# A hybrid decoder layer on one core: the sums of w_down's quarters put in other places, and the output projection's first two tiles written together

## The chip, the cores and the metric

The kernel runs on one core of a Trainium2 chip. The metric is device time in microseconds (us) of the whole launch; the kernel before was run three times. Every time in this document that is not a run's time comes from one profiled execution. Engines: TensorE (PE, matrix products), VectorE (DVE), ScalarE (ACT), GpSimd (POOL) and SyncE (SP). SP, ACT and POOL can each issue DMAs.

## The reference

One layer over 512 tokens of 2048 features, all in float32. Three sub-layers each add to the residual `x`; the last is a gated feed-forward layer with 5632 inner features:

```python
h = rms_norm(x, g_mix)
# h @ w_in -> sparse attention group (8 heads) and gated linear attention group (4 heads)
x = x + jnp.concatenate([o_nsa, o_gla], axis=-1) @ w_out
x = x + cross_attention(rms_norm(x, g_cross), rms_norm(mem, g_mem)) @ w_co   # 4 heads, 256 memory tokens
hf = rms_norm(x, g_ffn)
gg, uu = jnp.split(hf @ w_gu, 2, axis=-1)
return x + (jax.nn.silu(gg) * uu) @ w_down
```

## The kernel before

**Numbers and products.** Every float32 operand of a large product is split into a high and a low part (`split`, lines 153 to 160: a cast on ACT, a subtraction on DVE), and a product is three matmuls (`mm3`): high by high, high by low, low by high. A 128x512 matmul advances PE by about 0.23 us.

**Stages.** In order of time: keys and values of the memory (0 to 50 us); the input projection, its value columns first (`natural`, to 167 us), then tiles of 128 columns (`in_tile`), with the linear attention heads (`gla_head`) beside them, the compressed blocks (`compress_unit`, about 340 to 500 us) and the sparse heads (`nsa_head`, to 765 us); the output projection (`w_out`, 16 tiles, to 940 us); cross attention and its output `w_co` (to 1100 us); gate and up in eleven blocks of 512 inner features (1100 to 1930 us); down in four steps (to the end). The last two use a seven-product scheme of Strassen's kind, which is why sums of weight blocks are wanted.

**Weights.** In the first half `Weights` loads 1024 columns (512 KB) on SP into one of two raw tiles `w`, ACT casts it into one of three tiles `wh`, DVE makes `wl`. In gate and up a load is 768 KB (`weights_1`) or 512 KB (`weights_2`) into one of three tiles `raw`; DVE sums parts of it and ACT and DVE split it into tiles `qh` and `ql` (five and four). Each block of gate and up has two phases of eight steps `kp`; the finished block before is turned (`turn`, called after steps 2 and 4 of the second phase) and stored to DRAM by ACT's queue.

**Sums of w_down.** `w_down` lies in DRAM as quarters of 22 pieces of 512 KB. The tiles `td` in DRAM hold two sums of quarters per piece; the third step of down needs them first, at 2098 us. `add_quarters` makes them by DMA alone, on POOL's queue: a plain copy from DRAM to DRAM (line 143), then an accumulating copy onto it (line 141), 88 DMAs in all. Each waits for the last matmul written before its turn.

**What sets the order.** `Flows` is a list of generators for the small work. `flows.tick()` is called every few matmuls of the large projections; it counts `now` up and starts each entry of `marks` whose tick has come. The 88 sums have ticks from 70 to 576, 5.75 apart. The compiler's scheduler then orders each engine's instructions by priority; an engine takes its own in that order.

Of the kernel before, what the change touches and what calls it, by code (L numbers as in the profile page):

```python
# [19 lines left out]
KT = D // 128  # L20
# [8 lines left out]
NK = NF // 2  # L29
# [12 lines left out]

W_SUM, W_NORM, W_LEVEL = 3, 2, 2

FIRST_SUM, LAST_SUM = 70, 576

SV = {}
_n = 0
# [9 lines left out]
def hybrid_block(ctx: ExitStack, tc: tile.TileContext, x_t, mem_t, sv, cmat, umask, w_a, w_r67, w_v, w_vg, w_v3,  # L58
                 w_vsw, w_gk2, w_c1, w_c2, w_out, w_cq, w_ck, w_cv, w_co, w_gu, w_down, y_t):
    nc = tc.nc  # L60
    V, S, G, PE = nc.vector, nc.scalar, nc.gpsimd, nc.tensor
# [23 lines left out]
    def bank(tag):  # L85
        return psp.tile([128, 512], F32, name=tag, tag=tag, bufs={"mm": 3, "s": 2, "t": 2, "o": 1}[tag])
# [3 lines left out]
    def row(tag, dt=F32):  # L90
        return sb([128, 512], tag, BUFS[tag], dt)

    last_mm = [None]

    def mm(*args, **kw):
        last_mm[0] = PE.matmul(*args, **kw)  # L96

    class Flows:


        def __init__(self):
            self.now, self.live, self.marks = 0, [], []
# [27 lines left out]
    flows = Flows()  # L130
# [5 lines left out]
    def add_quarters(j, accumulate):  # L136
        dst = [td[i % NK][:, 1024 * (i // NK):1024 * (i // NK) + 1024] for i in (j, j - NK)]

        def go():
            if accumulate:  # L140
                i = G.dma_start(dst[0], dst[1] if j >= NK else w_down[1, j], accum_op=OP.add, max_dma_last_dim=2048)
            else:
                i = G.dma_start(dst[0], w_down[0 if j >= NK else 3, j % NK])
            tc.add_manual_dep(i.ins, last_mm[0].ins.name,
                              mybir.DependencyInfo(mybir.DependencyClass.Sync, mybir.DependencyReason.DATA),
                              reason="in its turn")
        return go

    for j in range(2 * NK):
        for k in range(2):  # L150
            flows.marks.append((FIRST_SUM + (2 * j + k) * (LAST_SUM - FIRST_SUM) // (4 * NK), add_quarters(j, k)))

    def split(hi, lo, src, gain=None):

# [7 lines left out]
    def split_row(src, gain=None, tag="X"):  # L162
        pair = row(tag, F32R), row(tag, F32R)
        split(*pair, src, gain)
        return pair

    class Weights:


        def __init__(self, src, cols, cut=1024, ahead=400, raws=(), step=1024):  # L170
            self.src, self.cols, self.cut, self.step, self.raws, self.parts = src, cols, cut, step, raws, []
            if ahead:
                with tc.high_priority(offset=ahead):
                    while len(self.parts) * cut < cols:
                        self.load()
# [22 lines left out]
    def mm3(ps, lhs, rhs, start, stop, again=False):  # L198
        mm(ps, lhs[0], rhs[0], start=start, stop=False, skip_group_check=again)
        mm(ps, lhs[0], rhs[1], start=False, stop=False, skip_group_check=again)  # L200
        mm(ps, lhs[1], rhs[0], start=False, stop=stop, skip_group_check=again)
# [13 lines left out]
    def vec(name, i=0, p=slice(0, 128)):  # L215
        a = SV[name][0] + i
        return vecs[p, a:a + 1]
# [65 lines left out]
    def project(w, src, cols=T, m=128):  # L283
        ps = bank("mm")
        for kt in range(len(src)):
            mm3(ps[:m, :cols], w(m * kt, m), src[kt], start=kt == 0, stop=kt == len(src) - 1)
            if kt % (2 * T // cols) == 1:
                flows.tick()
        return ps[:m, :cols]
# [106 lines left out]
    for kq in range(4):  # L396
# [6 lines left out]
        for k in range(4):  # L403
            kt = 4 * kq + k
# [3 lines left out]
            for h in range(4):  # L408
                mm3(acc_k[h // 2][:, MEM * (h % 2):MEM * (h % 2) + MEM], wk(512 * k + 128 * h, 128), mg[kt],
                    start=kt == 0 and h % 2 == 0, stop=kt == KT - 1 and h % 2 == 1)  # L410
# [53 lines left out]
    def in_tile(n):  # L464
        return project(Weights(w_a[n], 2048), xg)
# [176 lines left out]
    for h in range(GH):  # L642
        qk = []
        flows.start(gla_head(h, qk))
        q, k = row("Q"), row("Q")
# [107 lines left out]
    for b in range(2):  # L753
        for kv in range(2):
            pair = compress_blocks(us, "pe_k", 2 * b + kv)
            ps = in_tile(12 + 2 * b + kv)
# [7 lines left out]
    def nsa_head(h, ps):  # L764
# [89 lines left out]
        for b in range(2):  # L854
            pt = sb([128, 1280], "PH", PTB, F32R), sb([128, 1280], "PL", PTB, F32R)

            def turn(j):
                n = 128 * (NT - j)
                tp = bank("t")
                for i in range(j, NT):  # L860
                    PE.transpose(tp[:, 128 * (i - j):128 * (i - j) + 128],  # L861
                                 ps_[b][:, POFF[i] + 128 * j:POFF[i] + 128 * j + 128], ident)
                split(*part(pt, TOFF[j], n), tp[:, :n])

            def weigh(j):
                n = 128 * (NT - j)
                mm3(o[:, 128 * j:], part(vsw[j], 256 * b + 128 * kv, 128), part(pt, TOFF[j], n),
                    start=False, stop=b == 1 and j == NT - 1)

            turn(0)  # L870
            yield 2
            if b == 0:
                o = bank("o")
                mm(o, vc[:, 128 * kv:128 * kv + 128], pcs, start=True, stop=False)
            for j in range(1, NT):
                turn(j)
                weigh(j - 1)
                yield 2
            weigh(NT - 1)
# [32 lines left out]
    for n in IN_ORDER:  # L912
        ps = in_tile(16 + n)
# [5 lines left out]
    ps = [bank("mm") for _ in range(2)]  # L919
# [14 lines left out]
    mixp = [split_row(mix[k]) for k in MIX_ORDER]  # L934
# [4 lines left out]
        xs.append(t)  # L939
    ss = row("ss")  # L940
    x1g, x1d = [], []
    for m in range(KT):
        ps = project(Weights(w_out[m], 2048), mixp)
        V.tensor_add(xs[m], ps, xs[m])
        if m % 3 == 0:
            x1d.append(dram.tile([128, 512 * min(3, KT - m)], F32, name="x1", tag="x1", bufs=6))
        G.dma_start(x1d[-1][:, 512 * (m % 3):512 * (m % 3) + 512], xs[m])
        if m == 0:
            S.activation(ss, xs[m], AF.Square)
        else:  # L950
            sq = row("n")
            S.activation(sq, xs[m], AF.Square)
            V.tensor_add(ss, ss, sq)
        x1g.append(split_row(xs[m], vec("g_cross", m)))
# [74 lines left out]
    ps = project(Weights(w_cq[0], 2048), x1g)  # L1029
# [6 lines left out]
    def sb1(tag, dt=F32):  # L1036
        return pool1.tile([128, COLS2.get(tag, 512)], dt, name=tag, tag=tag, bufs=BUFS2[tag])
# [10 lines left out]
    def wide_weights(src, ahead):  # L1048
        with tc.high_priority(offset=ahead):
            raw = sb1("raw")  # L1050
            nc.sync.dma_start(raw, src)
            w = [split_cols(raw, 1024 * i, 1024) for i in range(2)]
        return lambda a, n: part(w[a // 1024], a % 1024, n)
# [11 lines left out]
    ws = [wide_weights(w_co[0], 40)]  # L1065
# [39 lines left out]
    for m in range(KT):  # L1105
        xr = x1[m]
        if m < 4:
            ps = ps4[m]
        else:
            ps = bank("mm")  # L1110
# [80 lines left out]
    def turn(hs, n, k, tag="s"):  # L1191
        def go():
            ps = [bank(tag), bank(tag)]
            for f in range(2):
                c = 256 * k + 128 * f
                for i in range(NT):
                    PE.transpose(ps[f][:, 128 * i:128 * i + 128], hs[i][:, c:c + 128], ident)  # L1197

            e, o, a, b = [sb1("T2") for _ in range(4)]
            S.copy(e, ps[0])  # L1200
            S.copy(o, ps[1])
            x, y = slice(0, 256), slice(256, 512)
            V.tensor_sub(a[:, x], e[:, y], o[:, y])
            V.tensor_sub(b[:, x], e[:, x], e[:, y])
            V.tensor_sub(a[:, y], a[:, x], e[:, x])
            V.tensor_add(b[:, y], o[:, x], a[:, y])
            d = hd[n // 3].rearrange("q (p c) -> q p c", p=7)
            c = 512 * (n % 3) + 256 * k
            S.dma_start(d[:, 0, c:c + 256], e[:, x])
            for p, t in ((1, o), (3, a), (5, b)):  # L1210
                S.dma_start(d[:, p:p + 2, c:c + 256], t.rearrange("q (p c) -> q p c", p=2))
        return go

    rc2 = []
# [2 lines left out]
    for n in range(NB):  # L1217
# [18 lines left out]
        if hs:  # L1236
            extra = {2: [turn(hs, n - 1, 0)], 4: [turn(hs, n - 1, 1)]}
# [278 lines left out]
```

## Time and profile before

| | |
|---|---|
| Runs | 2368.25, 2364.55, 2366.92 us; median 2366.92 |
| Profiled execution | 2365.85 us, its span 2364.1 us, mean granted clock 0.992 |
| PE busy | 2304.2 us, 97% of the span, 10954 matmuls |
| DVE, ACT, POOL busy | 71%, 50%, 6% |
| DMA | 421.34 MB, mean 178 GB/s |
| PE waits longest | 14.0 us at 1067 us, 8.1 at 782, 6.1 at 144, 5.7 at the start |

PE is busy nearly all of the time, so a shorter time must come from the stretches in which it idles, or in which its clock is at the lower of its two levels (2.4 and 1.2 GHz). The granted clock of a stretch is a mean: 0.83 over 20 us is 6.8 us at half speed.

### The profile page before, as it was taken

The numbers are of one execution on the slowest core, as the hardware profiler recorded it, in microseconds if no ns is written. First come the engines' busy times: TensorE is split into PE (matmuls) and PEld (weight loads), VectorE is DVE, ScalarE is ACT, GpSimd is POOL, SyncE is SP. The second block draws the span as 40 slices with busy tenths as digits, with TensorE's granted clock in tenths as the row PEclk, the third lists the DMA queues.
The fourth block names the chain that finished last, engine by engine and source line by source line (L and its number), as shares of the span: only waits on it lengthen the run. The fifth ranks groups of instructions, "written<-read, shape, count | busy, mean of one in ns | idle before, by whom it ended". The sixth has DMA issues, their size and how long they took to land.

```text
span 2364.1 us, 29618 instructions
## 1 busy us (share of the span) xinstructions
PE 2304.2 (97%) x10954; PEld 1915.9 (81%) x10954; DVE 1672.1 (71%) x2522; ACT 1185.6 (50%) x1787; POOL 133.4 (6%) x187
## 2 busy tenths in 40 slices
PE   8989999999999899979999999999999999999999
PEld 7788887878888788767888888888888888888887
DVE  6637776556778334478887888788878886785685
ACT  6623444446667223465554555455544556444542
POOL 0010111101112111010000000000000000000000
PEclk9999999999999999999999999999999999999999
DMA  7575446655546776265454455435544578676773
GB/s 240 159 184 139 120 133 181 181 147 143 148 121 192 222 193 185 75 196 170 145 177 144 142 174 169 158 130 171 174 155 132 170 277 327 234 249 230 251 249 143
DMA packets 131682, 421.34 MB, mean 178 GB/s; under 512 B 13488, under 2 KB 33968, under 8 KB 127312
## 3 DMA queue, kind: packets, MB, share of 16 engines
q1 hardware_dynamic: 82048, 325.05, 41.2%
q0 software_dynamic: 26064, 70.00, 12.8%
q10 hardware_dynamic: 23424, 24.39, 2.9%
q8 instruction: 86, 1.41, 0.2%
q14 instruction: 60, 0.49, 0.1%
HBM read 376.92 MB, written 84.67 MB: 195 GB/s over the span
## 4 chain that ended last, share of the span: by engine, by line
PE 88%; DMA 5%; DVE 3%; ACT 2%; issue 1%; SPq 0%; ACTq 0%; DVEq 0%; POOL 0%; POOLq 0%
PE mm L96 47%; PE t L96 15%; PE s L96 14%; PE o L96 10%; DVE wl L157 1%; ACT wh L156 1%; DMA w<-w_v 1%; PE s L1197 1%; PE t L861 1%; DMA w<-w_c 1%; DMA w<-w_a 1%; DMA st<-x_t 1%; DMA st<-spill 0%; ACT P L156 0%; DMA P<-h 0%
## 5 line engine op out<-in xcount | busy, mean ns | idle before, releaser
L156 ACT CAST qh<-raw 128x1024 fp32r<-128x1024 f32 (+1 forms) x520 | 505.7, 980 | 532.6 <-PE o L96 178.9
L157 DVE TENSOR_TENSOR ql<-raw,qh 128x1024 fp32r<-128x1024 f32 (+1 forms) x520 | 584.5, 1131 | 158.0 <-PE mm L96 50.4
L96 PE MATMUL mm<-qh,P 128*128 128x512 f32 x1540 | 535.7, 390 | 0.0
L96 PE MATMUL mm<-X,wh 128*128 128x512 f32 x1568 | 496.7, 397 | 10.1 <-ACT X L156 8.1
L96 PE MATMUL t<-qh,P 128*128 128x512 f32 x968 | 335.7, 392 | 14.0 <-ACT qh L156 14.0
L96 PEld LDWEIGHTS mm<-X,wh 128*128 128x128 f32 x1568 | 289.7, 189 | 66.3 <-ACT X L156 8.5
L96 PEld LDWEIGHTS mm<-qh,P 128*128 128x128 f32 x1540 | 289.5, 188 | 60.5 <-DVE T L1336 0.2
L157 DVE TENSOR_TENSOR wl<-w,wh 128x1024 fp32r<-128x1024 f32 (+2 forms) x154 | 184.5, 1200 | 183.1 <-ACT wh L156 182.5
L96 PE MATMUL mm<-X,wl 128*128 128x512 f32 x784 | 308.9, 394 | 1.8 <-DVE wl L157 1.7
L96 PE MATMUL mm<-ql,P 128*128 128x512 f32 x770 | 300.6, 390 | 0.8 <-DVE ql L157 0.8
L156 ACT CAST wh<-w 128x1024 fp32r<-128x1024 f32 (+2 forms) x154 | 158.2, 1029 | 258.9 <-PE mm L96 164.7
L96 PE MATMUL s<-qh,P 128*128 128x512 f32 x704 | 245.1, 393 | 0.7 <-ACT qh L156 0.7
L96 PEld LDWEIGHTS t<-qh,P 128*128 128x128 f32 x968 | 181.9, 188 | 51.5 <-ACT qh L156 14.5
L96 PE MATMUL t<-ql,P 128*128 128x512 f32 x484 | 188.5, 389 | 0.0
L96 PE MATMUL o<-qh,P 128*128 128x512 f32 x484 | 187.8, 390 | 0.0
L96 PEld LDWEIGHTS mm<-X,wl 128*128 128x128 f32 x784 | 148.1, 189 | 34.5 <-DVE wl L157 3.5
L96 PEld LDWEIGHTS mm<-ql,P 128*128 128x128 f32 x770 | 144.8, 188 | 31.7 <-DVE ql L157 1.9
L96 PEld LDWEIGHTS s<-qh,P 128*128 128x128 f32 x704 | 132.5, 189 | 28.4 <-ACT qh L156 1.7
L96 PE MATMUL s<-ql,P 128*128 128x512 f32 x352 | 138.2, 393 | 0.1
L1139 DVE TENSOR_TENSOR raw<-raw 128x1024 f32<-128x1024 f32 x88 | 106.5, 1220 | 16.9 <-DMA raw<-w_gu 16.8
L96 PE MATMUL mm<-wh,X 128*128 128x512 f32 (+1 forms) x320 | 101.1, 367 | 7.7 <-ACT wh L156 6.5
L96 PEld LDWEIGHTS o<-qh,P 128*128 128x128 f32 x484 | 91.1, 188 | 18.8
(395 smaller groups left out, 3099.9 us busy)
## 6 DMA issues: line engine op xcount, KB each, us to landing
raw<-w_gu SPq DMA_DIRECT2D x88, 768.0 KB, 4.2
raw<-w_gu SPq DMA_DIRECT2D x88, 512.0 KB, 3.5
raw<-w_down SPq DMA_DIRECT2D x88, 512.0 KB, 4.6
td<-w_down POOLq DMA_DIRECT2D x66, 512.0 KB, 5.4
w<-w_a SPq DMA_DIRECT2D x60, 512.0 KB, 4.4
raw<-td SPq DMA_DIRECT2D x22, 1024.0 KB, 4.8
h<-T ACTq DMA_DIRECT2D x66, 256.0 KB, 3.7
w<-w_out SPq DMA_DIRECT2D x32, 512.0 KB, 4.5
```

What stands on the lines that cost most here:

```text
L96: last_mm[0] = PE.matmul(*args, **kw)
L156: S.copy(hi, src)
L157: V.tensor_sub(lo, src, hi)
L861: PE.transpose(tp[:, 128 * (i - j):128 * (i - j) + 128], ps_[b][:, POFF[i] + 128 * j:POFF[i] + 128 * j + 128], ident)
L1139: V.tensor_sub(raw[:, 0:1024], raw[:, 0:1024], raw[:, 512:1536])
L1197: PE.transpose(ps[f][:, 128 * i:128 * i + 128], hs[i][:, c:c + 128], ident)
```

## The change

The 88 sums no longer stand at even distances. 70 of them go into four stretches of ticks: 24 in 112 to 222, 6 in 254 to 300, 22 in 330 to 420 and 18 in 470 to 576. The other 18 are issued in gate and up, one by each of the first 18 calls of `turn`: a pair (copy, then accumulating copy) for each of nine blocks. Such a sum waits for the turn's first subtraction on DVE instead of a matmul. Besides, the first two tiles of the output projection are written as 15 steps of the first, 15 of the second, then the last step of each.

```diff
-FIRST_SUM, LAST_SUM = 70, 576
+SUMS = ((112, 222, 12), (254, 300, 3), (330, 420, 11), (470, 576, 9))
...
-        def go():
+        def go(when=None):
...
-            tc.add_manual_dep(i.ins, last_mm[0].ins.name,
+            tc.add_manual_dep(i.ins, (when or last_mm[0]).ins.name,
...
-    for j in range(2 * NK):
-        for k in range(2):
-            flows.marks.append((FIRST_SUM + (2 * j + k) * (LAST_SUM - FIRST_SUM) // (4 * NK), add_quarters(j, k)))
+    sums = [add_quarters(j, k) for j in range(2 * NK) for k in range(2)]
+    for a, b, n in SUMS:
+        flows.marks += [(a + i * (b - a) // (2 * n), sums.pop(0)) for i in range(2 * n)]
...
+            self.done = False
...
+
+    ws = [Weights(w_out[m], 2048) for m in range(2)]
+    begun = [bank("mm") for _ in ws]
+    for m in (0, 1, 0, 1):
+        for kt in range(KT - 1) if not ws[m].done else (KT - 1,):
+            mm3(begun[m], ws[m](128 * kt, 128), mixp[kt], start=kt == 0, stop=kt == KT - 1)
+            if kt % 2:
+                flows.tick()
+        ws[m].done = True
     for m in range(KT):
-        ps = project(Weights(w_out[m], 2048), mixp)
+        ps = begun[m] if m < 2 else project(Weights(w_out[m], 2048), mixp)
...
-            V.tensor_sub(a[:, x], e[:, y], o[:, y])
+            h = V.tensor_sub(a[:, x], e[:, y], o[:, y])
...
+            if sums:
+                sums.pop(0)(h)
```

POOL's order where the sparse heads end and the output projection begins, before; L959 and L960 reload the keys and values of the memory for cross attention, L947 stores the first sums of the residual:

```order
L930 DMA KS<-spill 128x512
L959 DMA st<-spill 128x512
L960 DMA st<-spill 128x512
L143 DMA td<-w_down 128x1024 x2
L141 DMA td<-td 128x2x512 x2
L143 DMA td<-w_down 128x1024
L959 DMA st<-spill 128x512
L960 DMA st<-spill 128x512
L141 DMA td<-td 128x2x512
L143 DMA td<-w_down 128x1024
L947 DMA x_7170<-KV 128x512 x2
```

The same place on POOL now (these lines are 10 further down in the changed kernel):

```order
L903 DMA st<-spill 128x512
L931 DMA KS<-spill 128x512
L969 DMA st<-spill 128x512
L970 DMA st<-spill 128x512
L969 DMA st<-spill 128x512
L970 DMA st<-spill 128x512
L143 DMA td<-w_down 128x1024
L957 DMA x_7215<-KV 128x512 x2
L141 DMA td<-td 128x2x512
L957 DMA x_7215<-KV 128x512
```

The five sums that stood between the two pairs of reloads are gone from there.

The end of POOL's order now, from the reloads of the residual (L1096) to the last instructions; before, nothing followed the fifteen accumulating DMAs onto `hT`:

```order
L1096 DMA P<-x_8224 128x512
L1139 DMA hT<-C 128x512 x15
L143 DMA td<-w_down 128x1024
L141 DMA td<-td 128x2x512
L143 DMA td<-w_down 128x1024
L141 DMA td<-td 128x2x512
L143 DMA td<-w_down 128x1024
L141 DMA td<-td 128x2x512
L143 DMA td<-w_down 128x1024
L141 DMA td<-td 128x2x512
```

Nine such pairs stand there, the only work of POOL in gate and up.

PE's order at the output projection before: `mm_7119`, `mm_7189` and `mm_7261` are the banks of the first, second and third tile, `X_7070` is the high part of the last of the 16 inputs:

```order
L96 MATMUL mm_7189<-X_7066,wl_7185 128x512
L96 MATMUL mm_7261<-X_7010,wh_7250 128x512
L96 MATMUL mm_7261<-X_7011,wh_7250 128x512
L96 MATMUL mm_7261<-X_7010,wl_7251 128x512
L96 MATMUL mm_7261<-X_7014,wh_7250 128x512
L96 MATMUL mm_7261<-X_7015,wh_7250 128x512
L96 MATMUL mm_7261<-X_7014,wl_7251 128x512
L96 MATMUL mm_7261<-X_7018,wh_7250 128x512
L96 MATMUL mm_7119<-X_7070,wh_7114 128x512
L96 MATMUL mm_7189<-X_7070,wh_7184 128x512
```

The same place on PE now; the banks are `mm_7115`, `mm_7116` and `mm_7243`, the last input `X_7054`:

```order
L96 MATMUL mm_7116<-X_7050,wl_7111 128x512
L96 MATMUL mm_7243<-X_6994,wh_7232 128x512
L96 MATMUL mm_7243<-X_6995,wh_7232 128x512
L96 MATMUL mm_7243<-X_6994,wl_7233 128x512
L96 MATMUL mm_7243<-X_6998,wh_7232 128x512
L96 MATMUL mm_7243<-X_6999,wh_7232 128x512
L96 MATMUL mm_7243<-X_6998,wl_7233 128x512
L96 MATMUL mm_7243<-X_7002,wh_7232 128x512
L96 MATMUL mm_7115<-X_7054,wh_7098 128x512
L96 MATMUL mm_7116<-X_7054,wh_7110 128x512
```

Nothing has moved on PE here but the buffers' numbers. Over the whole program the orders of PE, ACT and SP are the same in both kernels, and DVE's differs in one neighbouring pair.

## Rows read from the trace of the kernel before

**Rows 1.** The page: the chain that ended last, shares by engine.

```profile
PE 88%; DMA 5%; DVE 3%; ACT 2%; issue 1%; SPq 0%; ACTq 0%; DVEq 0%; POOL 0%; POOLq 0%
```

**Rows 2.** Busy time by stretch: length, engines, granted clock, DMA share, GB/s.

```profile
130.00:150.00 20.00, 13.87 (x101) 13.69 (x100) 7.83 (x23) 6.28 (x10) 2.75 (x4) 0.83 0.75 178
365.00:410.00 45.00, 39.47 (x176) 30.34 (x176) 29.91 (x44) 20.32 (x33) 3.46 (x4) 0.96 0.63 171
470.00:490.00 20.00, 16.91 (x87) 13.55 (x85) 9.15 (x10) 9.09 (x11) 2.23 (x3) 1.00 0.73 219
500.00:700.00 200.00, 200.00 (x1058) 169.10 (x1057) 141.06 (x424) 130.16 (x289) 23.65 (x33) 1.00 0.51 132
770.00:790.00 20.00, 11.93 (x46) 9.43 (x45) 8.20 (x11) 6.13 (x9) 2.92 (x4) 0.83 0.80 242
```

**Rows 3.** Timeline of PE: start, length, instruction, idle time before it.

```profile
144.16 0.42 PE L489 MATMUL t<-ident,q 128*96 128x128 f32 x1 [6.13 <-DVE gates L478]
...
399.14 0.66 PE L96 MATMUL t<-ht,st 128*128 128x64 f32 x4 [2.75 <-DVE ht L699]
...
781.98 2.07 PE L96 MATMUL mm<-X,wh 128*128 128x512 f32 x4 [8.07 <-ACT X L156]
```

**Rows 4.** The chain in order of time: start, length, what.

```profile
132.35 9.00 DMA w<-w_v
...
388.30 7.67 DMA w<-w_a
...
764.69 11.33 DMA st<-spill
```

**Rows 5.** DMA queues and issues: count, size, median us to landing.

```profile
q0 software_dynamic: 26064, 70.00, 12.8%
...
raw<-w_gu SPq DMA_DIRECT2D x88, 512.0 KB, 3.5
...
w<-w_a SPq DMA_DIRECT2D x60, 512.0 KB, 4.4
...
w<-w_out SPq DMA_DIRECT2D x32, 512.0 KB, 4.5
...
st<-spill POOLq DMA_DIRECT2D x12, 256.0 KB, 5.5
```

**Rows 6.** Timeline of POOL, the sums.

```profile
114.44 0.54 POOL L143 DMA_DIRECT2D td<-w_down  x1 [31.41 <-PE s L96]
...
344.85 0.56 POOL L143 DMA_DIRECT2D td<-w_down  x1 [7.92 <-PE s L96]
...
761.38 2.38 POOL L141 DMA_DIRECT2D td<-td  x2 [6.72 <-DMA td<-w_down]
```

**Rows 7.** Timeline of ACT before the wait at 782 us.

```profile
776.05 0.62 ACT L156 CAST P<-st 128x512 fp32r<-128x512 f32 x1 [9.28 <-DMA st<-spill]
```

**Rows 8.** The chain at the same matmuls of three blocks of gate and up.

```profile
1502.65 2.72 PE mm L96 x12
...
1580.65 2.72 PE mm L96 x12
...
1659.98 2.72 PE mm L96 x12
```

**Rows 9.** Landings of line 1149's loads, stretch 1580 to 1608.

```profile
DMA to landing us min/median/max: 3.5/4.2/5.1
```

**Rows 10.** Landings of line 1149's loads, stretch 1502 to 1530.

```profile
DMA to landing us min/median/max: 3.1/3.3/4.3
```

**Rows 11.** Timeline of DVE and PE in gate and up.

```profile
1213.79 1.23 DVE L1139 TENSOR_TENSOR raw<-raw 128x1024 f32<-128x1024 f32 x1 [1.44 <-DMA raw<-w_gu]
1214.93 0.42 DVE L1203 TENSOR_TENSOR T<-T,T 128x256 f32<-128x256 f32 x1
...
1605.70 1.23 DVE L1139 TENSOR_TENSOR raw<-raw 128x1024 f32<-128x1024 f32 x1 [2.49 <-DMA raw<-w_gu]
...
1617.18 0.73 PE L96 MATMUL s<-qh,P 128*128 128x512 f32 x2 [0.71 <-ACT qh L156]
```

## The prediction

> **What bounds the kernel now.** I read the chain first: PE has 88% of it, DMA 5% [rows 1]. So the kernel is a stream of matmuls, and only PE's idle time and its half-speed time can be won. Next I read PE's timeline for idle time and the busy time by stretch for what each hole is worth. Four holes in the first half have a DMA behind them [rows 2]:
>
> - 130 to 150 us: idle 20.00 − 13.87 = 6.1 us, and a granted clock of 0.83, which is 0.17 × 20 = 3.4 us of lost work: 9.5 us.
> - 365 to 410: 5.5 us idle, 0.04 × 45 = 1.8 us of clock: 7.3 us.
> - 470 to 490: 3.1 us idle at full clock.
> - 770 to 790: 8.1 us idle, 3.4 us of clock: 11.5 us.
>
> Together 31.4 us. Then I asked the chain what stands before each hole. Before the first, a 512 KB weight load that takes 9.00 us; in the second, one of 7.67; before the last, a reload of 256 KB that takes 11.33 [rows 4]. The medians of such transfers are 4.4 and 5.5 us [rows 5]. At these places POOL's queue has sums in flight: they begin at 114.44 us [rows 6] and go on at an even pace. So the holes are loads slowed by the sums. The named releasers (`gates`, `ht`, a cast) only stand behind the late load in the order of DVE or ACT [rows 3, 7].
>
> **Where the sums go.** Before, the n-th sum has tick 70 + 506n/88; counting POOL's rows of lines 141 and 143 turns ticks into times. The 27th (tick 219) is at 344.85 us [rows 6]. So the stretches are about 155 to 340 us, 400 to 465, 525 to 714 and 785 to 917 us, and no sum is issued at 114 to 150, 345 to 400, 465 to 520 and 720 to 780 us. These are the holes, each with a few us ahead of it. 18 sums move out of the first half.
>
> **Hole by hole.**
>
> - First: with the 9.00 us load at 4.4, the gates come 4.6 us earlier, and the load before it, also beside a sum, gives the rest. I take all of the 6.1 but 0.3, and all of the clock, since even the third hole, 3.1 us in pieces, left it at 1.00 [rows 2]: 9.2 us.
> - Second: the loads of the compressed blocks come in pairs into two raw tiles, a loop as long as a landing and a split, so some of the wait may be the loop's own. The hole at 399 us (2.75 us, [rows 3]) hangs on the 7.67 us load, 3.3 over the median. I leave 0.8 us: 6.5 us. Lower bound: that hole and the clock alone, 4.5.
> - Third: the last accumulating sum of the second stretch is issued at tick 292, just ahead of 460 us, and still overlaps the loads there. I leave 0.8: 2.3 us.
> - Fourth: ACT waits 9.28 us for the reload [rows 7], and the norm of the last head is queued behind it. From the landing at 764.69 + 11.33 = 776.02 to PE's restart at 781.98 are 6.0 us of casts and small operations [rows 3, 4], which stay. PE ran dry at 781.98 − 8.07 = 773.9. The reload can't start earlier: its tile is freed by the splits of the last gates. Without sums ahead of it I give it its median, 5.5 us: landing 770.2, restart 776.2, hole 2.3 us. The gain is 5.8 and the clock's 3.4: 9.2 us. Ten loads of the residual are in flight there as well; were the reload to land in 8 us, the gain would be 3.3, with the clock 6.7 or less.
>
> By the Trainium skill (DMA: Bandwidth & Descriptors, the section on queues, rings and completion order) an engine takes turns between queues but drains one queue's ring in order, so a reload suffers fully from sums ahead in POOL's own queue and only half from SP's loads. The trace agrees as far as two accumulating sums are issued at 761.38 us [rows 6], 3.3 us ahead of the slow reload.
>
> Sum: 9.2 + 6.5 + 2.3 + 9.2 = 27.2 us.
>
> **The pair of tiles.** It does nothing. PE's order already had both tiles up to their fifteenth input, and part of the third, ahead of the first matmul on the last input, and the order is the same now. The splits' orders are the same too. What stays at the fourth hole stays in spite of it. Cost and gain 0, since no engine's sequence differs.
>
> **What the sums cost elsewhere.** In the fuller stretches (24 in place of 18, 22 in place of 16) a sum adds DMA time where PE has no idle time at all and the DMA share is 0.51 [rows 2]. POOL's queue moved 70.00 MB in 12.8% of 2364 us of all sixteen engines [rows 5], 4.3 us per MB, or 2.3 us for a sum of 0.52 MB; six more in 190 us add 0.07 to the share. Bounds: 0, and a hole like the third in each (6 us). I take 2, near the row at 500 to 700.
>
> In gate and up the sums cost most. Each pair is issued while the last loads of the second phase and the first of the next block's first phase are in flight; DVE takes the next block's first raw tile at 1213.79 us, after 1.44 us of waiting for it, and the second sum is released one instruction later, at 1214.93 [rows 11]. One block shows what a delay does here. At 1580 to 1608 us the four loads of the second phase land in 4.2 us (median) instead of 3.3 [rows 9, 10]; DVE waits 2.49 us for the next block's first load instead of the 1.44 above, PE 0.71 us at 1617 [rows 11], and the block takes 1659.98 − 1580.65 = 79.33 us instead of 1580.65 − 1502.65 = 78.00 [rows 8]: 1.33 us. Beside sums, 512 KB of `w_out` land in 4.5 us, and of `w_gu`, without sums, in 3.5 [rows 5]; so a sum does about that, but to two loads of a block instead of four or five. I take 0.6 us for each of nine blocks, 5.5 us. Bounds: 0 (nothing lands earlier for it), and the whole 4.6 us of a pair in front of the loads, 41 us; the late block is the near row. Behind a sum on POOL only the next sum is queued, and nobody waits for that before 2098 us.
>
> By the Trainium skill (same page, the section that issuing engines are not separate DMA queues) DMAs of POOL run on the same 16 engines as SP's and interleave with them, so a sum is never free for a load beside it. That speaks against the 18 sums in gate and up; it is the mechanism of the second and third rival.
>
> **Forecast.** −27.2 + 2 + 5.5 = −19.7 us. The profiled execution took 2365.85 us, 1.1 under the median of 2366.92; from the median that is 2347 us, own range 2340 to 2354.
>
> **Rivals.**
>
> 1. *The holes close by half.* The loads slow each other (pairs in the second hole, the residual's ten loads in the fourth). For it: DMA shares of 0.63 to 0.80 there [rows 2]; against it: each slow one has a sum issued within a few us. 13.6 − 7.5 = 6 us faster: 2361. 13%.
> 2. *Each block of gate and up pays what the late block paid.* 1.33 × 9 = 12 us: 13 us faster, 2354. For it: the loads have no slack; against it: only two meet a sum. 16%.
> 3. *Slower: the pairs set the pace of gate and up.* The whole pair stands in front of the loads between two blocks, 41 us: −27 + 2 + 41 = 16 us slower, 2383. It decides from (27.2 − 2)/9 = 2.8 us a block. For it: DVE's wait passes straight to PE in the late block; against it: the second sum comes after that block's first load has landed. 5%.
> 4. *1 and 2 together*: 13.6 − 2 − 12, no change: 2367. 6%.
>
> The forecast has 60%. What a measurement of this kernel can tell from no change is 0.2%, 4.7 us. Faster by more: 60 + 16 and most of rival 1, 0.86. Within: rival 4 and the rest of rival 1, 0.09. Slower: 0.05. The range from 2334 (gate and up at no cost, holes wholly closed, a few us more) to 2362 leaves out rivals 3 and 4 and a little below.
>
> **What would show it.** Right: no PE idle time over 1.5 us and no clock below 1.00 at 130 to 150; the weight loads there near 4.4 us; the hole at the output projection's last input near 2 us, its reload near 5.5; PE's order unchanged; blocks of gate and up 78.6 us apart. Wrong: a reload that lands in 8 us or more without sums; blocks of 80 us or more with DVE waiting for `w_gu`; new idle time at 525 to 714 us with a load beside a sum before it.

## The result, and the profile after

The changed kernel takes 2352.15 us (median of 4 runs, 2347.40 to 2355.05), the kernel before 2367.43 beside it (4 runs). The ratio is 0.9933, 95% interval 0.9917 to 0.9949: 15.3 us faster. Forecast were 2347 us (19.7 us faster) and a range of 2334 to 2362. The profiled execution is the slowest of the four: 2355.05 us, span 2353.2; against the profiled execution before it is 10.8 us faster, and the traces below add up to that.

The page after: the queue of the sums, the chain by engine, and the issues.

```profile
q0 software_dynamic: 26064, 70.00, 13.0%
...
PE 85%; DVE 5%; DMA 5%; ACT 2%; issue 2%; ACTq 0%; SPq 0%; DVEq 0%; POOLq 0%
...
w<-w_a SPq DMA_DIRECT2D x60, 512.0 KB, 3.7
```

The kernel is faster, yet PE's share of the chain falls from 88% to 85% and DVE's rises from 3% to 5% [rows 1]. So there is a new wait, and this row alone says that something was given back. POOL's queue moved the same 70.00 MB, so no sum is missing. `w_a`, whose loads stood in the second hole, lands in 3.7 us where it took 4.4 [rows 5].

The stretches of the four holes, widened to the left as the work now comes earlier, the stretch at 500 to 700, and one at the front (95 to 115). Columns as in [rows 2].

```profile
95.00:115.00 20.00, 17.24 (x74) 14.45 (x73) 9.02 (x17) 8.72 (x16) 0.00 (x0) 0.83 0.13 38
...
120.00:150.00 30.00, 29.95 (x234) 29.77 (x233) 12.00 (x28) 8.24 (x13) 0.00 (x0) 1.00 0.38 126
345.00:410.00 65.00, 64.87 (x307) 52.41 (x306) 44.24 (x63) 31.34 (x49) 3.43 (x5) 1.00 0.50 154
455.00:495.00 40.00, 39.47 (x200) 31.92 (x199) 21.53 (x27) 17.22 (x25) 0.00 (x0) 1.00 0.46 145
...
500.00:700.00 200.00, 200.00 (x1053) 168.73 (x1052) 147.24 (x441) 132.49 (x296) 31.18 (x43) 1.00 0.57 151
...
745.00:790.00 45.00, 42.79 (x191) 34.79 (x191) 23.50 (x32) 18.30 (x27) 7.26 (x11) 1.00 0.73 216
```

Three holes are gone: PE is idle 0.05, 0.13 and 0.53 us where it was idle 6.1, 5.5 and 3.1, all at a clock of 1.00, and the DMA share at the first fell from 0.75 to 0.38 [rows 2]. Of the fourth 2.21 us are left, at full clock. The stretch at 500 to 700, with 43 of POOL's instructions in place of 33, has no idle time at all.

PE's timeline after at three places: start, length, instruction, idle time before it.

```profile
100.21 0.70 PE L96 MATMUL s<-n,ones_r 128*128 128x512 f32 x1 [2.76 <-ACT n L156]
...
760.62 1.22 PE L96 MATMUL mm<-X,wh 128*128 128x512 f32 x4 [2.21 <-ACT X L156]
...
1443.29 0.73 PE L96 MATMUL s<-qh,P 128*128 128x512 f32 x2 [0.76 <-ACT qh L156]
```

The fourth hole is 2.21 us where it was 8.07 [rows 3]. In the chain of waits the reload in front of it is this piece:

```profile
749.12 5.53 DMA st<-spill
```

5.53 us in place of 11.33 [rows 4]. The third row of the timeline is new: such a stop stands at the start of eight of the blocks of gate and up, and there was none before but one. What a block takes is read best from the transposes of the turns. One row holds their count, min/median/max length in ns, and the start of the first and the last. Before:

```profile
L1197 PE MATMUL s<-ident,C x160: 270/273/274, 1202.5 to 1916.2; 128*128 128x128 f32 x160
```

After:

```profile
L1207 PE MATMUL s<-ident,C x160: 270/273/273, 1180.1 to 1906.1; 128*128 128x128 f32 x160
```

That is the whole account. The first turn comes 1202.5 − 1180.1 = 22.4 us sooner; from the first to the last take 726.0 us in place of 713.7, 12.3 us longer; from the last to the end (2364.1 − 1916.2 = 447.9, now 447.1) 0.8 us shorter. −22.4 + 12.3 − 0.8 = −10.9, the difference of the spans.

Between the turns PE's columns read, before and after, from the first turn's start to the tenth's:

```profile
1202.50:1906.40 703.90, 703.12 (x3170) 582.48 (x3169) 574.17 (x703) 358.31 (x451) 0.00 (x0) 1.00 0.48 159
```

```profile
1180.10:1896.30 716.20, 707.95 (x3170) 580.84 (x3169) 573.35 (x702) 358.30 (x450) 15.29 (x18) 1.00 0.52 170
```

The same 3170 matmuls, a clock of 1.00 in both; PE is idle 8.25 us instead of 0.78, and its busy time is 4.8 us longer. So the trace books part of the loss as matmuls that last longer: looking for idle time alone one would have found 7.5 of the 12.3 us.

Who waits there? The waits of DVE for loads in 1180 to 1890 us (us in total, times, longest): before

```profile
DVE raw L1139 <- DMA raw<-w_gu: 15.4, 11, 2.5
```

and after

```profile
DVE raw L1149 <- DMA raw<-w_gu: 28.4, 10, 3.5
```

13.0 us more, on the loads of the first phase. One boundary between blocks in the chain of waits after, 1410 to 1440 us:

```profile
1419.94 4.21 DMA raw<-w_gu
1424.17 0.04 DVE raw L1160
1425.50 6.23 DMA raw<-w_gu
1431.82 1.22 DVE raw L1149
```

and POOL's timeline there:

```profile
1421.78 0.56 POOL L143 DMA_DIRECT2D td<-w_down  x1 [66.43 <-DVE T L1213]
1433.68 1.14 POOL L141 DMA_DIRECT2D td<-td  x1 [11.34 <-DVE T L1213]
```

The plain copy of the pair is issued 3.7 us ahead of the next block's first load, which takes 6.23 us, and DVE stands still for it. In the chain of 1180 to 1890 us loads of `w_gu` (of both phases) have 6.3% after; before, no load is in it. The accumulating sum comes at 1433.68, after that load has landed (1425.50 + 6.23 = 1431.73). What I could not tell from this trace is which of the two, or the mere count of them, costs the 1.37 us a block.

### The profile page after: what moved, and what is told of

The parts are those of the page before. It is cut to its first block, busy times and chain, and to the rows that moved or that the text cites. A ratio compares the mean times of both kernels' runs of the same rounds, so it can differ in the third digit from the quotient of the medians.

```text
span 2353.2 us, 29618 instructions
## 1 busy us (share of the span) xinstructions
PE 2305.2 (98%) x10954; PEld 1912.2 (81%) x10954; DVE 1673.3 (71%) x2522; ACT 1185.8 (50%) x1787; POOL 133.0 (6%) x187
## 4 chain that ended last, share of the span: by engine, by line
PE 85%; DVE 5%; DMA 5%; ACT 2%; issue 2%; ACTq 0%; SPq 0%; DVEq 0%; POOLq 0%
PE mm L96 46%; PE t L96 15%; PE s L96 14%; PE o L96 9%; DMA raw<-w_gu 2%; DVE ql L157 2%; DMA raw<-w_down 1%; DMA st<-x_t 1%; PE t L862 1%; DVE wl L157 1%; PE s L1207 0%; ACT wh L156 0%; ACT qh L156 0%; DVE raw L1149 0%; ACT P L156 0%
## 5 line engine op out<-in xcount | busy, mean ns | idle before, releaser
L96 PEld LDWEIGHTS t<-qh,P 128*128 128x128 f32 x968 | 181.8, 188 | 52.5 <-ACT qh L156 15.3
L96 PEld LDWEIGHTS t<-ql,P 128*128 128x128 f32 x484 | 90.9, 188 | 19.6 <-DVE ql L157 1.4
```

## The experiments

All ratios are against the kernel before, run on the same chip in the same comparison. "Turns" is the time from the first to the last of the 160 transposes: 713.7 us before, 726.0 after.

**e1_no_late**: nothing is summed in gate and up.

```
-            if sums:
-                sums.pop(0)(h)
...
```

> This kernel leaves out the 18 sums of gate and up: nine pieces of w_down are used without the second quarter, read from w_down in place of td. Theory A (the pairs cost 1.3 to 1.7 us a block, 12 us in all, since each block grew from 78.0 to 79.3 us and more): blocks go back to 78.0 us, first to last turn 704 us as before the change instead of 716, median near 2340 us, ratio to the kernel before near 0.988. Rival B (the blocks grew because gate and up now starts at another time, or by something else that the change moved): blocks stay at 79.3 and the time at 2352.

2344.14 us (2341.96 to 2346.38), ratio 0.9895 [0.9879, 0.9911]. The turns:

```profile
L1207 PE MATMUL s<-ident,C x160: 270/273/273, 1181.6 to 1894.1; 128*128 128x128 f32 x160
```

712.5 us, 13.5 less than in the changed kernel, and the first turn stands where it stood (1181.6 and 1180.1). So the nine pairs cost the 12 to 13 us, and all of it inside the blocks. This kernel leaves 18 sums out, so by itself it doesn't say whether they cost by their number or by their place.

**e2_phase1**: the same nine pairs, issued behind steps 4 and 6 of each block's first phase instead of in its turns.

```
-            if sums:
-                sums.pop(0)(h)
...
+        late = {kp: [sums.pop(0)] for kp in (4, 6)} if n and sums else {}
...
-              AHEAD if n else 40, {}, fence)
+              AHEAD if n else 40, late, fence)
```

> All 88 sums are made, but the nine pairs of gate and up are issued in the first phase of a block (behind the matmuls of steps 4 and 6) instead of in the turns. Theory A1 (it is the place: at the turn a sum meets the stores of the turn and the next block's first two loads, which land 1.6 and 2.0 us later and have no slack): blocks 78.0 to 78.3 us, median near 2341 us, ratio near 0.989. Rival A2 (any sum in gate and up costs its DMA time, wherever it stands): blocks at 79.3 or more, 2352 us or more.

2345.95 us (2342.59 to 2350.52), 0.9903 [0.9888, 0.9919]. Turns:

```profile
L1207 PE MATMUL s<-ident,C x160: 270/272/275, 1178.8 to 1893.9; 128*128 128x128 f32 x160
```

715.1 us, 10.9 less than after. All the bytes are moved, and nearly nothing is lost: it is the place that costs. The landings in 1260 to 1900 us (loads of the first phase, the turn's stores, the copy) say the same. Before:

```profile
raw<-w_gu SPq DMA_DIRECT2D x64, 768.0 KB, 4.2
...
h<-T ACTq DMA_DIRECT2D x48, 256.0 KB, 3.1
```

After:

```profile
raw<-w_gu SPq DMA_DIRECT2D x64, 768.0 KB, 4.9
...
h<-T ACTq DMA_DIRECT2D x48, 256.0 KB, 5.0
td<-w_down POOLq DMA_DIRECT2D x8, 512.0 KB, 6.3
```

With the pairs in the first phase:

```profile
raw<-w_gu SPq DMA_DIRECT2D x64, 768.0 KB, 4.1
...
h<-T ACTq DMA_DIRECT2D x53, 256.0 KB, 3.4
td<-w_down POOLq DMA_DIRECT2D x7, 512.0 KB, 4.2
```

The last column is the median landing: the loads 4.1 instead of 4.9, the turn's stores 3.4 instead of 5.0, the copy itself 4.2 instead of 6.3. The median over all eight loads of a phase doesn't decide, though: in e5 below it is 4.2 for the loads, and the time is as long as after. At the turn three kinds of transfers meet: the stores of `h`, the copy and the next block's loads.

**e5_copy_in_turn** and **e6_acc_in_turn**: only one of the pair stays in the turn, the other goes behind step 6 of the first phase. With the copy in the turn:

```
-            if sums:
+            if sums and k == 0:
...
+        late = {6: [sums.pop(0)]} if n > 1 and sums else {}
...
```

> The plain copy of each late pair stays in the turn after step 2; the accumulating one is moved behind step 6 of the next first phase. Theory C (the copy is what hurts: it goes out 4 us before the next block's first load, holds up that load and the turn's stores, and these hold up the second load): blocks 79.0 to 79.5 us, about 2352 us. Theory D (the accumulating sum hurts, which moves more bytes): blocks 78.0 to 78.4, about 2343 us.

2353.54 us (2351.50 to 2357.36), 0.9934 [0.9918, 0.9950], and turns of 725.8 us: no better than after. The row of who waited for the first phase's loads (DVE, us and times, 1260 to 1900):

```profile
  DVE raw L1149: 27.3, 8
```

With the accumulating sum in the turn:

```
-            if sums:
+            if sums and k:
...
+        late = {6: [sums.pop(0)]} if n and sums else {}
...
```

> The other way round: the copy goes out behind step 6 of a block's first phase, the accumulating sum stays in the turn after step 4 of its second phase. Theory C: blocks 78.0 to 78.4 us, the first two loads of a block land in 4.2 to 4.7 us, about 2344 us. Theory D: blocks 79.0 to 79.5, about 2352 us.

2346.02 us (2345.68 to 2346.99), 0.9901 [0.9886, 0.9915]. Its row of who waited, and its turns:

```profile
  DVE raw L1149: 11.5, 10
...
L1207 PE MATMUL s<-ident,C x160: 270/272/273, 1182.8 to 1895.6; 128*128 128x128 f32 x160
```

712.8 us, as without any sum (712.5 in e1). The same row of who waited in the changed kernel, and before:

```profile
  DVE raw L1149: 25.0, 8
...
  DVE raw L1139: 13.4, 9
```

In this stretch eight blocks begin, each with eight loads in its first phase, and DVE waits 8 to 10 times: about once a block. The traces tell for which load. These are means over the nine blocks that a pair meets, in us:

| | before | after | e5 | e6 |
|---|---|---|---|---|
| Landing of the first load | 4.3 | 5.8 | 6.2 | 4.0 |
| of the second | 5.0 | 6.4 | 6.1 | 5.0 |
| of the third | 4.4 | 5.4 | 4.3 | 6.4 |
| of the fourth | 5.2 | 5.3 | 5.0 | 5.8 |
| DVE waits for the first | 1.6 | 3.1 | 3.4 | 1.2 |
| for the second | 0.1 | 0.1 | 0.0 | 0.2 |

Of a first phase DVE waits for the first load, hardly for the second, and for no other. So it is the plain copy that costs: with it in the turn the first load lands 1.5 us later (after) than before, DVE waits 1.5 us longer for it, and the block takes 1.37 us longer. The second load is late too, but it has landed by the time DVE comes to it. The accumulating sum in e6 makes the third and fourth load late, for which DVE doesn't wait, and costs nothing. The stores aren't what hurts: in e6 they land in 4.2 us (median) in place of 3.1 before, and nothing is lost. Not every wait of DVE counts: for the loads of the second phase it waits 30.7 us in e1 and 39.2 in e9 below (1180 to 1890 us), and the turns take 712.5 and 712.4. Two things are not separated: the kind of transfer and its place. An accumulating sum in the copy's place was not run.

**e3_unpair**: the two output tiles are written one after the other again.

```
-    ws = [Weights(w_out[m], 2048) for m in range(2)]
-    begun = [bank("mm") for _ in ws]
...
-        ps = begun[m] if m < 2 else project(Weights(w_out[m], 2048), mixp)
+        ps = project(Weights(w_out[m], 2048), mixp)
```

> The output projection's tiles are written one after the other again; all else as in the changed kernel. Theory: the order of PE is the same with and without it, so nothing changes: idle time before the last input's matmuls near 2.2 us, the stage from there on the same, time within 0.2% of the changed kernel (2347 to 2357 us). Rival (the pair of tiles is what closed the 8 us hole): the hole is 8 us again and the time 6 to 11 us longer.

2358.66 us (2355.97 to 2361.80), 0.9952 [0.9934, 0.9970]. The hole:

```profile
761.00 1.22 PE L96 MATMUL mm<-X,wh 128*128 128x512 f32 x4 [2.45 <-ACT X L156]
```

2.45 us with tiles apart, 2.21 with the pair, by the same releaser. The time is above what I expected (2347 to 2357), so I ran the changed kernel once more as **e8_again**.

> The changed kernel once more, beside the kernels of this call and to compare with the one whose tiles are written one after the other (2358.66 us, ratio 0.9952, 0.9934 to 0.9970). Theory (the pair of tiles does nothing): ratio to the kernel before between 0.993 and 0.996, overlapping that one's; hole at the output projection 2 to 2.7 us. Rival (the pair is worth some us): ratio 0.9933 or less and clear of 0.9952.

2355.08 us (2349.92 to 2359.02, 6 runs), 0.9939 [0.9924, 0.9954], a hole of 2.42 us. The intervals of the two overlap over most of their length, the instructions stand in one order, and the hole is the same: the pair of tiles is not shown to be worth anything. The two profiled executions agree up to the first turn (1183.2 us in e3, 1183.6 in e8); of the 2.7 us between their spans (2359.9 and 2357.2) 2.1 lie behind the last turn, far from the pair.

**e4_refill**: four of the nine pairs of sums of the fourth stretch go back into the gap before the output projection.

```
-SUMS = ((112, 222, 12), (254, 300, 3), (330, 420, 11), (470, 576, 9))
+SUMS = ((112, 222, 12), (254, 300, 3), (330, 420, 11), (424, 466, 4), (484, 576, 5))
```

> Eight of the 18 sums of the last stretch of ticks are moved to ticks 424 to 466, where the changed kernel has none. Theory (the hole at the output projection came from sums ahead of the reload of 256 KB in POOL's queue): the reload lands in 8 us or more instead of about 5, the hole before the last input's matmuls is 5 us or more instead of 2.2, half speed for 6.8 us behind it, time 6 to 9 us over the changed kernel. Rival (the hole closed for another reason, the pair of tiles or the earlier start): hole and time as in the changed kernel.

2360.93 us (2358.84 to 2369.82), 0.9972 [0.9956, 0.9989]: about half of the gain is gone. POOL's timeline, ACT's and PE's:

```profile
748.89 1.15 POOL L141 DMA_DIRECT2D td<-td  x1 [4.12 <-PE t L862]
749.84 0.80 POOL L969 DMA_DIRECT2D st<-spill  x1
750.42 0.76 POOL L143 DMA_DIRECT2D td<-w_down  x1
...
759.26 0.62 ACT L156 CAST P<-st 128x512 fp32r<-128x512 f32 x1 [7.32 <-DMA st<-spill]
...
765.36 2.08 PE L96 MATMUL mm<-X,wh 128*128 128x512 f32 x4 [6.28 <-ACT X L156]
```

The reload stands between two sums, ACT takes it up only at 759.26 us, 9.4 us after its issue, and the hole is back at 6.28 us. The clock of 755 to 775 us is 0.83 again.

**e10_refill_early**: sums in the two early gaps (72 to 110, 222 to 254), fewer in the stretches.

```
+SUMS = ((72, 110, 4), (112, 222, 8), (222, 254, 3), (254, 300, 3), (330, 420, 8), (470, 576, 9))
```

> Eight sums of the changed kernel's first stretch go to ticks 72 to 110 and six of the third to ticks 222 to 254, so the places of the first two holes are filled again. Theory (sums beside the loads make the holes): the weight loads at 130 to 145 us land in 7 to 9 us and PE idles there 4 us or more, with the clock at half speed behind it; 4 us or more of idle time at 345 to 400 us; time 10 to 16 us over the changed kernel. Rival (the holes went because of something else, such as the other order on POOL): no hole there, time as the changed kernel.

2373.00 us (2370.89 to 2376.07), 1.0031 [1.0017, 1.0045]: slower than the kernel before, and some 20 us over the changed one, more than the 10 to 16 expected. Its stretches, and its chain before the first hole:

```profile
120.00:150.00 30.00, 23.06 (x169) 22.89 (x168) 9.09 (x24) 6.71 (x11) 5.16 (x6) 0.91 0.82 195
345.00:410.00 65.00, 59.21 (x268) 47.16 (x268) 42.21 (x57) 32.69 (x50) 7.94 (x11) 0.93 0.67 184
```

```profile
127.41 7.03 DMA w<-w_v
...
136.87 8.30 DMA w<-w_v
```

Both holes are back (6.9 and 5.8 us idle, both with a lowered clock), the first behind slow `w_v` loads as in [rows 4]. Seven pairs in the gaps cost 20 us. By the Trainium skill (DMA: Bandwidth & Descriptors, the section that issuing engines are not separate DMA queues) DMAs that POOL issues share the engines with SP's. The slower loads here agree; that it need not cost time, the next run shows.

**e7_all_first**: no sums in gate and up, all in the same four stretches of the first half.

```
+SUMS = ((112, 222, 15), (254, 300, 4), (330, 420, 14), (470, 576, 11))
```

> All 88 sums stand in the four stretches of the first half (30, 8, 28 and 22 of them), none in gate and up. Theory (a fuller stretch costs next to nothing, since PE has no idle time there at a DMA share near 0.5): blocks of gate and up 78.0 us, no new hole over 1 us before 740 us, about 2342 us, ratio near 0.989. Rival (the fuller stretches bring holes of their own, which is what the pairs in gate and up avoid): new holes of 3 us and more, time 2348 us or more.

2343.89 us (2343.04 to 2345.24), 0.9911 [0.9895, 0.9928]. The stretch in which I had feared a new hole:

```profile
500.00:700.00 200.00, 200.00 (x1055) 168.85 (x1055) 146.01 (x445) 131.73 (x293) 36.43 (x49) 1.00 0.62 163
```

A DMA share of 0.62 and not one idle us. The stretches could have held all 88 sums; the nine pairs need not have gone to gate and up.

**e9_reload_late**: e2, and the reloads for the cross attention wait for the last matmul of the first two output tiles.

```
+    both = last_mm[0]
...
-        G.dma_start(ckt[i], memkv["k", i])
-        G.dma_start(cv[i], memkv["v", i])
+        for t, d in ((ckt[i], memkv["k", i]), (cv[i], memkv["v", i])):
+            tc.add_manual_dep(G.dma_start(t, d).ins, both.ins.name, ...
```

> The sums as in the kernel with the pairs in the first phase; besides, the four reloads for cross attention wait for the last matmul of the first two output tiles, so ACT no longer stands at them when the last head's norm is due. Theory (the hole of 2.2 us that is left is still that reload in ACT's order): no hole before the last input's matmuls, no half speed there, time 2 to 4 us under that kernel's 2346, ratio near 0.989. Rival (the head's norm itself ends that late, or ACT now stands at the reload a little later, in front of a weight's cast): hole stays at 2 us or moves into the first tiles, time 2344 to 2352 us.

2341.48 us (2338.99 to 2344.05), 0.9877 [0.9860, 0.9895], the best of all and below both kernels. PE from 755 to 775 us, first in e2, then here:

```profile
755.00:775.00 20.00, 17.37 (x70) 13.82 (x69) 11.33 (x15) 8.16 (x12) 3.89 (x6) 0.91 0.64 191
```

```profile
755.00:775.00 20.00, 20.00 (x89) 16.12 (x88) 9.34 (x12) 6.05 (x10) 5.31 (x8) 1.00 0.76 225
```

The 2.63 us of hole and the clock of 0.91 are both gone, though the DMA share is higher and the reloads now land in 10.5 us (median of four): PE no longer waits behind them. So what was left of the fourth hole was not the landing as such, but a cast of the reload that stands in ACT's order in front of the norm that PE waits for. PE's share of the chain is 93% now. How much of the time this gives is not shown: the intervals of e2 and e9 overlap, and in the profiled executions the first turn stands at 1179.6 us here and at 1178.8 in e2. What e9 wins at 760 us it loses again at 905 to 955 us, where its clock is 0.90 and that of e2 1.00. Two profiled executions of one kernel, the changed one, differ there as well (0.97, and 0.90 in e8).

## Why the prediction was right, and where it was not

*The holes: right.* Three of four are gone and the fourth has 2.2 us left (forecast 2.3), its reload lands in 5.53 us (forecast 5.5). Idle and clock of the four were worth 31.4 us; 2.9 of idle time are left (0.05 + 0.13 + 0.53 + 2.21), so 28.5 came back, and 27.2 were forecast. The cause is shown from both sides: sums put back into the gaps bring back the late loads, the holes and the clock (e4, e10). Rival 1, that the loads slow each other, falls. The way to the 2.3 us was right too: from the reload's landing to PE's restart it is 6.0 us, as forecast (749.12 + 5.53 = 754.65 to 760.62). No run separates whether the reload was late because the sums stood ahead of it in POOL's own queue, as the prediction had it, or because of any transfers beside it.

*The pair of tiles: right.* The hole is the same without it (e3). That the interval of e3 lies a little higher than that of e8 leaves room for at most a few us, with no row that would show where.

*Fuller stretches: mis-sized.* 2 us were forecast, and e7, with still more sums there, has no idle time in 500 to 700 us and the first turn at 1181.7 us: nothing that can be seen. The share of DMA may rise from 0.51 to 0.62 where loads have time.

*Gate and up: the step that failed.* Forecast were 0.6 us a block, 5.5 us in all; measured are 12.3 us over the nine, 1.37 a block. I halved the 1.33 us of the late block [rows 8] because "only two" loads meet a sum, and held for it that the second sum comes after the first load has landed [rows 11]. The second half of that was right: the accumulating sum costs nothing (e6). The first was not: what counts is not how many loads a transfer meets but which. In e6 two loads of a block are late as well, at no cost. The copy meets the first load of the block, the one for which DVE already waited (1.44 us) [rows 11], and what this load is late goes into the block nearly whole: 1.5 us later, 1.37 us longer. The rows held this: of the late block's 1.33 us, 2.49 − 1.44 = 1.05 are DVE's longer wait for this one load [rows 11], so there was nothing to share out among five. That is rival 2 in size, and in mechanism as far as the first load goes: that one has no slack, the other loads of the first phase have. Its time of 2354 us is nearer to the 2352 measured than the forecast's 2347. Rival 3 (41 us) falls.

*The sum again, with sizes as measured:* −28.5 + 0 + 12.3 = −16.2 us. All of these sizes come from the profiled executions, and those differ by only 10.8 us, so it proves little that the medians differ by 15.3. One reason shows in the first row of the stretches: at 95 to 115 us the clock is 0.83 after, 0.17 × 20 = 3.4 us of lost work that the profile before doesn't have. The other 2 us I can't place; the four runs of this kernel alone lie 7.7 us apart.

*The clock.* I had assumed that a hole of up to 3 us leaves it at 1.00, from the third hole, which came in pieces. That is too simple, as the last section shows; the forecast got all of the fourth hole's clock back, and in the first profile of the changed kernel that is so (2.21 us, clock 1.00). In the second, e8, a hole of 2.42 us took the clock at 755 to 775 us to 0.91, which is 1.8 us; so there this part of the forecast held by luck of the execution.

## What to carry to other kernels

Place side traffic by the slack of the loads that it will meet, not by the mean DMA share: the same eighteen transfers cost 12 us at the boundary between blocks, where a copy goes out just ahead of the first load of a block, whose delay reaches PE, and next to nothing in the middle of a phase or in a stretch with a DMA share of 0.6. Before a cost is shared out by "how many" loads are hit, look in the waits for the one that is already waited for, and whether that wait reaches the engine that sets the time. And where a hole stays after its load is fast, look at what stands behind the load in the order of an in-order engine, and move that load behind the hole.

## What the runs showed of the hardware

- A hole of 2 to 3 us can lower the granted clock, and need not. After 2.76 us of idle time at 100 us it was 0.83 in the 20 us around it, and PE worked at its lower level, 1.2 GHz in place of 2.4: three matmuls of one group take 1.28 us there, and took 0.69 before. Before the change, with 2.30 us there:

```profile
95.00:115.00 20.00, 17.70 (x100) 15.47 (x99) 9.37 (x18) 9.15 (x17) 0.54 (x1) 1.00 0.21 61
```

At 760 us 2.21 us left it at 1.00 (after), but 2.04 us took it to 0.91 (e6, 755 to 775 us), as did 2.63 (e2, above) and 2.42 in the changed kernel's second profile (e8):

```profile
755.00:775.00 20.00, 17.58 (x71) 13.93 (x70) 10.11 (x13) 8.20 (x12) 2.86 (x4) 0.91 0.70 210
```

So the length of such a hole alone doesn't decide, and it can cost 1.8 to 3.4 us beside its own length. Whether the drop at 100 us has to do with the change is open: up to 114 us the programs are the same, but all eleven profiled executions of kernels with the sums moved have it (holes of 2.33 to 3.14 us, a clock of 0.83 or 0.91 at 95 to 115 us), and the only one of the kernel before has not.

- A copy from DRAM to DRAM and the loads beside it slow each other: the first load of a block lands in 4.0 us without the copy in the turn (e6) and in 6.2 with it (e5), means over nine blocks. The copy of 512 KB lands in 4.2 us (e2, behind step 4) or 5.6 us (e6, behind step 6) in a first phase and in 6.3 beside the turn's stores and the next loads (after), medians of 1260 to 1900 us.
